# A hybrid SSD / short-convolution / MoE layer on one core: scale 2 and gate 2 summed on VectorE, their neighbours and the second C block moved in TensorE's order

## The chip, the cores and the metric

The kernel runs on one core of a Trainium2 chip. The time is the device time of the one launch, in microseconds (us), as the median of several runs. The profile is one more execution, recorded by the hardware profiler. In all rows PE is TensorE (matmul), PEld its weight load, DVE is VectorE, ACT is ScalarE, POOL is GpSimd, SP is SyncE, on whose queue (SPq) the large loads are issued.

## What is computed

One layer over 256 latent tokens (`x`) and 256 context tokens, model width 1024, all in float32. What matters here:

```
mod_x = (silu(c) @ w_mod + b_mod).reshape(6, D)       # 1024 -> 6 x 1024: shift 1, scale 1, gate 1, shift 2, scale 2, gate 2
hx    = rmsnorm(x) * (1 + scale1) + shift1
ox    = concat(bidirectional SSD scan, gated short conv)(hx @ w_in) @ w_out
x     = x + gate1 * ox
x     = x + gate2 * moe(rmsnorm(x) * (1 + scale2) + shift2)      # top 4 of 32 experts, w_gate_up 1024x2048, w_down 1024x1024 each
out   = rmsnorm(x)
```

`w_mod` is 1024 x 6144. It is used in three phases of 2048 columns: phase 0 holds shift 1 and scale 1, phase 1 gate 1 and shift 2, phase 2 scale 2 and gate 2. Gate 1, shift 2, scale 2 and gate 2 are wanted only behind the scan.

## The kernel before

The kernel runs in stages. Up to about 60 us the inputs are normalized and modulated and the first in-projection blocks are made. Then come the blocks of the scan's operands: X0 to X7 (`x_block`), B, and two C blocks (`c_block`, lines 531 to 536), each a projection with the weights split into a high and a low part (`split`, line 281: the high part a cast on ScalarE, the low part a subtraction on VectorE or GpSimd), 24 products on TensorE (`gemm`, line 291), and a convolution with silu (`conv_silu`, line 306: one operation on ScalarE, two additions on VectorE that read PSUM, a silu on ScalarE). The scan has 16 steps (the loop at line 676): step s is head pair s // 2 in direction s % 2. In each, `decays(s + 1)` makes the decay rows on TensorE, their exponentials on ScalarE, `mx` on VectorE and `ex` on GpSimd, and `outputs(s)` uses those of the step before on TensorE and, on odd steps, adds the result to `yb` on VectorE (line 614). Work that has nothing to do with the scan is put between as filler: the short-convolution blocks (`sc_block`, 12 of 24 in steps 2 to 13) and the modulation vectors. Behind the scan come the other 12 short-convolution blocks, the Z blocks, the out-projection, the router, and then the 32 experts, whose 12 MB of weights each are streamed through slots of 1 MB.

The modulation vectors of phases 1 and 2 are made by the generator `mods` (line 192). Each of its first eight `next` calls loads 128 rows of `w_mod` (1 MB, `load_mod`, line 187, in one of two slots of `ringm`) and multiplies them with 128 values of silu(c) on TensorE: four products 128x32 by 128x512, put side by side in one PSUM tile (line 202). The ninth call is the tail: 8 products with one column turn one half of the row into a column per partition (`pq`, line 211), and 2 of 512 columns copy the other half to all partitions (`pgate`, line 217). `m1` makes gate 1 and shift 2, `m2` scale 2 and gate 2. Calls of m1: three ahead of `token_steps` (line 649), two behind `scores(1)` (line 669), and, in the scan, one in each step from 2 to 5. Calls of m2: one in each step from 6 to 14.

What sets the order: TensorE's order is that of the program, written out (`manual_schedule`, line 405), from the end of the first projections to the end of the out-projection. The other engines and the DMA queues are put in order by the framework's planner, which goes by program order and by when it expects an operation to be ready; a queue, once planned, runs strictly in order. `tc.issue_after(i)` puts what is traced in it behind instruction i on that engine. A tile with a tag and `bufs=n` shares n buffers with all tiles of that tag, and waits until one is free. Those that matter: `proj` (PSUM, 2 buffers, the output of each projection block from X2 on), `cv` (2, a convolution's sum), `cx` (2, the X block in rows of channels, read by the token transposes), `ringm` (2 slots of 1 MB).

Silus from X1 on are held back behind `weighted`, the exponential at line 459, so that ScalarE's function table is loaded once.

Of the kernel before, what the change touches and what calls it, by code (L numbers as in the profile page):

```python
# [8 lines left out]
F32 = mybir.dt.float32  # L9
# [5 lines left out]
ALU = mybir.AluOpType  # L15
# [3 lines left out]
P = 128  # L19
D = 1024  # L20
KD = D // P
# [41 lines left out]
def body(ctx, tc, x, ctx_in, vectors_in, w_mod, b_mod, w_in, w_out, w_router, b_router, w_gate_up, b_gate_up,  # L63
         w_down, b_down, final_g, out, taps=None):
    nc = tc.nc
    taps = taps or {}

    def tap(name, ap):
        if name in taps:
            nc.gpsimd.dma_start(taps[name], ap)  # L70

    def dram(ap, offset, pattern):
        return bass.AP(tensor=ap.tensor, offset=ap.offset + offset, ap=pattern)
# [118 lines left out]
    def mods(ph, gate, gate_first, col):  # L192

        acc = ps.tile([P, 512], F32, tag="pm", bufs=1, name=f"pmod{ph}")
        rows = mp.tile([P, 512], F32, tag="sacc", name=f"rows{ph}")
        nc.gpsimd.memset(rows, 0.0)
        nc.gpsimd.dma_start(rows.rearrange("(j p) n -> j p n", p=32)[:, 0, :],
                            dram(b_mod, ph * 2048, [[512, 4], [1, 512]]))
        for k in range(KD):
            w = load_mod(ph, k)  # L200
            for j in range(4):
                nc.tensor.matmul(acc[32 * j:32 * j + 32, :], ct[:, k, :], w[:, 512 * j:512 * j + 512],
                                 start=(k == 0), stop=(k == KD - 1), skip_group_check=True)
            if k == KD - 1:
                nc.vector.tensor_add(rows, rows, acc)
            yield
        jg, jc = (0, 2) if gate_first else (2, 0)
        pq = ps.tile([P, 512], F32, tag="misc", bufs=2, name=f"pq{ph}")
        for q in range(KD):
            j = jc + q // 4  # L210
            nc.tensor.matmul(pq[:, q:q + 1], rows[:, (q % 4) * P:(q % 4 + 1) * P], ident[:, 32 * j:32 * j + 1],
                             start=True, stop=True)
        nc.vector.tensor_copy(col, pq[:, 0:KD])
        for hf in range(2):
            j = jg + hf
            pg = ps.tile([P, 512], F32, tag="misc", bufs=2, name=f"pgate{ph}_{hf}")
            nc.tensor.matmul(pg, ident[:, 32 * j:32 * j + 1].to_broadcast([P, P]), rows, start=True, stop=True)
            nc.scalar.copy(gate[:, hf, :], pg)
        yield

# [257 lines left out]
    g1 = mp.tile([P, 2, 512], F32, tag="g1", name="g1")  # L478
    g2 = mp.tile([P, 2, 512], F32, name="g2")
    m1 = mods(1, g1, True, sh2)  # L480
    m2 = mods(2, g2, False, gs2)
    yb = mp.tile([P, 8, T], F32, tag="x28", name="yb")
    ws = t2a.tile([P, 2, NT, NH, HD], F32, tag="big8", name="ws")
    xdt = t2a.tile([P, 2, NT, NH, HD], F32, tag="xd8", name="xdt")
# [46 lines left out]
    def c_block(g):  # L531
        if g == 0:
            wcol["C"] = load_cols(C0, "C")
        pp = proj(wcol["C"], g, T, f"C{g}", nc.vector)
        cch[g] = t2s.tile([P, T], F32, name=f"c{g}")
        conv_silu(pp, 10 + g, T, cch[g][:, None, :], weighted.ins)
# [56 lines left out]
    py = [None]  # L593

    def outputs(s_, mxs, exs):
        hp, d_ = s_ // 2, s_ % 2
        g = hp // 4
        ja, jb = (0, 1) if d_ == 0 else (1, 0)
        half = slice(P, T) if d_ == 0 else slice(0, P)
        xd = xdt[:, d_]  # L600
        if d_ == 0:
            py[0] = ps.tile([P, T], F32, tag="py", bufs=1, name=f"py{hp}")
        for hh in range(2):
            nc.tensor.matmul(py[0][64 * hh:64 * hh + 64, :], xd[:, ja, 2 * hp + hh, :], mxs[hh][:, 0:256],
                             start=(d_ == 0), stop=False, skip_group_check=True)
        for hh in range(2):
            nc.tensor.matmul(py[0][64 * hh:64 * hh + 64, half], xd[:, jb, 2 * hp + hh, :], mxs[hh][:, 256:384],
                             start=False, stop=False, skip_group_check=True)
        for hh in range(2):
            h_ = 2 * hp + hh  # L610
            nc.tensor.matmul(py[0][64 * hh:64 * hh + 64, :], h0[d_][g][:, (h_ % 8) * HD:(h_ % 8 + 1) * HD], exs[hh],
                             start=False, stop=(d_ == 1), skip_group_check=True)
        if d_ == 1:
            nc.vector.tensor_add(yb[:, hp, :], yb[:, hp, :], py[0])


    cs, cv = {}, {}
# [28 lines left out]
    context_b(1)  # L646
    x_block(3)
    c_block(0)
    for _ in range(3):
        next(m1)  # L650
    token_steps()
    x_tokens(0)
    x_tokens(1)
    decay_rows()
    c_block(1)
    x_block(4)
    x_tokens(2)
    x_tokens(3)
# [7 lines left out]
    last_silu = x_block(7)  # L666
    x_tokens(6)
    scores(1)
    for _ in range(2):
        next(m1)  # L670
    x_tokens(7)
    sc_steps = [(kind, 2 * q + half) for q in range(4) for kind in "CUB" for half in range(2)]
    fill = [lambda: context_state(0, 1), lambda: context_state(1, 1)]
# [2 lines left out]
    for s_ in range(16):  # L676
        if fill:
            fill.pop(0)()
        if s_ >= 2:
            next(m1 if s_ < 6 else m2, None)  # L680
        done_ = step
        if s_ < 15:
            step = decays(s_ + 1)
        outputs(s_, *done_)
    tap("y", yb)
    sa.close()
    scp = ctx.enter_context(tc.tile_pool(name="scp", bufs=1, reuse_waits="tile"))
# [7 lines left out]
    def sc_parts():  # L695
        while sc_done:
            ti, v_ = sc_done.pop(0)
            nc.scalar.copy(sc[0][:, ti, :], v_)
            nc.gpsimd.tensor_tensor(sc[1][:, ti, :], v_, sc[0][:, ti, :].bitcast(F32), op=ALU.subtract)

    sc_parts()
    for a in sc_steps[12:]:
        sc_block(*a)
        sc_parts()


    yhl = [scp.tile([P, 2, 4, T], F32R, tag=("ya", "yb")[g], name=f"y{g}") for g in range(2)]
# [770 lines left out]
```

## Time and profile before

| | us |
|---|---|
| median of 3 runs | 1299.02 (1299.01 to 1303.77) |
| the profiled execution | 1297.97 |
| its span, first to last instruction | 1296.2 |

| engine | busy, us | share of the span |
|---|---|---|
| TensorE | 1170.4 | 90% |
| VectorE | 435.6 | 34% |
| ScalarE | 258.4 | 20% |
| GpSimd | 122.1 | 9% |

The mean granted TensorE clock is 0.970. 466 MB are moved, 360 GB/s in the mean. The shares are means over stages of different kinds: up to 340 us TensorE works on projections and the scan while loads come and go, behind that the experts' weights are streamed. The rows further down are read by stage.

### The profile page before, as it was taken

The numbers are of one execution on the slowest core, as the hardware profiler recorded it, in microseconds if no ns is written. First come the engines' busy times: TensorE is split into PE (matmuls) and PEld (weight loads), VectorE is DVE, ScalarE is ACT, GpSimd is POOL, SyncE is SP. The second block draws the span as 40 slices with busy tenths as digits, with TensorE's granted clock in tenths as the row PEclk, the third lists the DMA queues.
The fourth block names the chain that finished last, engine by engine and source line by source line (L and its number), as shares of the span: only waits on it lengthen the run. The fifth ranks groups of instructions, "written<-read, shape, count | busy, mean of one in ns | idle before, by whom it ended". The sixth has DMA issues, their size and how long they took to land.

```text
span 1296.2 us, 16117 instructions
## 1 busy us (share of the span) xinstructions
PE 1170.4 (90%) x6113; PEld 538.1 (42%) x6113; DVE 435.6 (34%) x878; ACT 258.4 (20%) x510; POOL 122.1 (9%) x140
## 2 busy tenths in 40 slices
PE   7989999999899989899898878998977899888985
PEld 6666767988433322243222223422321243223221
DVE  5475454654432432213324212222321113212222
ACT  5444544554400010010001001000100010001002
POOL 1232333426100100000000000000000000000000
PEclk9999999999899999999999989999998999899998
DMA  9743468786499999999999999999999999999994
GB/s 324 266 164 130 164 228 280 257 294 270 170 417 415 416 415 417 416 416 417 417 416 416 416 416 416 416 416 416 416 416 417 417 416 417 416 416 416 416 415 186
DMA packets 111841, 466.12 MB, mean 360 GB/s; under 512 B 9576, under 2 KB 40424, under 8 KB 76944
## 3 DMA queue, kind: packets, MB, share of 16 engines
q1 hardware_dynamic: 111504, 464.37, 90.4%
q8 instruction: 50, 0.82, 0.3%
q0 software_dynamic: 256, 0.67, 0.1%
q14 instruction: 31, 0.25, 0.1%
HBM read 463.97 MB, written 1.05 MB: 359 GB/s over the span
## 4 chain that ended last, share of the span: by engine, by line
PE 77%; DMA 13%; DVE 6%; ACT 2%; issue 1%; SPq 1%; POOL 0%; ACTq 0%; DVEq 0%; POOLq 0%
PE pdn L1123 8%; PE pg L1111 8%; DMA gu<-in_w_gate_up_dram 8%; PE pl L1111 7%; PE pg L1191 6%; PE pc L1087 6%; PE pgl L1160 6%; PE pdn L1175 4%; PE pdn L1198 3%; DMA dn<-in_w_down_dram 3%; PE pd L999 2%; DMA wim<-in_w_mod_dram 2%; PE pgl L1154 1%; PE pat L1080 1%; PE ppX L293 1%; PE ppX L294 1%
## 5 line engine op out<-in xcount | busy, mean ns | idle before, releaser
L1111 PE MATMUL pg<-gu,xe 128*64 128x512 f32 x480 | 152.6, 610 | 1.5 <-DMA gu<-in_w_gate_up_dram 1.5
L1111 PE MATMUL pl<-gu,xe 128*64 128x512 f32 x480 | 149.3, 599 | 0.0
L1054 ACT ACTIVATE s<-a 128x512 f32<-128x512 f32 (+1 forms) x35 | 19.1, 545 | 591.0 <-DVE a L1053 591.0
L1087 PE MATMUL pc<-ye,gt 64*128 64x512 f32 (+1 forms) x248 | 100.3, 647 | 27.6 <-DVE ye L1134 14.5
L1160 PE MATMUL pgl<-gu,xe 128*32 128x512 f32 x896 | 114.4, 617 | 11.8 <-DMA gu<-in_w_gate_up_dram 11.8
L1123 PE MATMUL pdn<-dn,at 128*64 128x512 f32 x480 | 117.3, 634 | 6.9 <-ACT at L1082 6.8
L1089 DVE TENSOR_TENSOR x<-x,pc 128x512 f32<-128x512 f32 x124 | 81.7, 684 | 123.1 <-PE pc L1087 123.1
L1053 DVE TENSOR_SCALAR a<-pg 128x512 f32<-128x512 f32 x21 | 14.5, 690 | 216.0 <-PE pg L1111 150.5
L1191 PE MATMUL pg<-gu,xe 128*128 128x512 f32 x192 | 83.9, 592 | 0.0
L1134 DVE TENSOR_TENSOR ye<-g2s,pdn 128x512 f32<-128x512 f32 x29 | 19.9, 687 | 153.1 <-PE pdn L1123 106.3
L1313 POOL DMA_DIRECT2D fg<-in_final_g_dram x1 | 0.6, 591 | 746.4 <-PE pd L999 746.4
L1087 PEld LDWEIGHTS pc<-ye,gt 64*128 64x128 f32 (+1 forms) x248 | 28.5, 186 | 100.5 <-DVE x L1089 42.9
L1111 PEld LDWEIGHTS pl<-gu,xe 128*64 128x64 f32 x480 | 42.2, 138 | 67.1 <-issue 66.8
L1175 PE MATMUL pdn<-dn,at 128*32 128x512 f32 x448 | 63.4, 674 | 6.5 <-ACT at L1082 5.4
L1111 PEld LDWEIGHTS pg<-gu,xe 128*64 128x64 f32 x480 | 38.5, 138 | 69.9 <-issue 60.1
L1123 PEld LDWEIGHTS pdn<-dn,at 128*64 128x64 f32 x480 | 33.9, 145 | 72.8 <-issue 58.0
L1160 PEld LDWEIGHTS pgl<-gu,xe 128*32 128x32 f32 x896 | 24.9, 111 | 88.4 <-issue 56.7
L1191 PEld LDWEIGHTS pg<-gu,xe 128*128 128x128 f32 x192 | 35.8, 190 | 41.6 <-issue 40.9
L999 PE MATMUL pd<-oh,hr 128*128 128x256 f32 (+1 forms) x256 | 41.9, 305 | 5.6 <-DVE xe L1001 5.0
L1198 PE MATMUL pdn<-dn,at 128*128 128x512 f32 x96 | 43.5, 601 | 0.0
L999 PEld LDWEIGHTS pd<-oh,hr 128*128 128x128 f32 x256 | 34.2, 198 | 20.9 <-DVE xe L1001 10.7
L1067 DVE TENSOR_SCALAR go<-io,gp 128x128 f32<-128x128 f32 x56 | 18.6, 369 | 67.0 <-PE pgo L1071 67.0
(406 smaller groups left out, 1635.0 us busy)
## 6 DMA issues: line engine op xcount, KB each, us to landing
gu<-in_w_gate_up_dram SPq DMA_DIRECT2D x256, 1024.0 KB, 19.9
dn<-in_w_down_dram SPq DMA_DIRECT2D x127, 1024.0 KB, 20.0
wm<-in_w_mod_dram SPq DMA_DIRECT2D x16, 1024.0 KB, 5.2
wim<-in_w_mod_dram SPq DMA_DIRECT2D x8, 1024.0 KB, 11.6
wo<-in_w_out_dram SPq DMA_DIRECT2D x8, 1024.0 KB, 5.1
wiX<-in_w_in_dram SPq DMA_DIRECT2D x4, 1024.0 KB, 9.9
wiSC<-in_w_in_dram SPq DMA_DIRECT2D x4, 1024.0 KB, 6.4
wiSU<-in_w_in_dram SPq DMA_DIRECT2D x4, 1024.0 KB, 6.5
```

The source lines that it names most:

```text
L999: nc.tensor.matmul(pd[:, :width], hr[n // 2][:, n % 2, k * P:(k + 1) * P], oh[:, n % 2, :], start=(n == 0), stop=(n == 3))
L1054: nc.scalar.activation(s, a, AF.Sigmoid, scale=ALPHA)
L1067: nc.vector.tensor_scalar(go if cap == P else go.rearrange("p (a s) -> p a s", s=cap), io1 if cap == P else io1[:, None, 0:cap].to_broadca ...
L1087: nc.tensor.matmul(pc_, lhs, rhs, start=True, stop=True)
L1089: return nc.vector.tensor_add(ysl, ysl, pc_).ins
L1111: nc.tensor.matmul(pp[64 * hf:64 * hf + 64, :], xk[k], gu[k][:, i * FF + hf * 512:i * FF + hf * 512 + 512], start=False, stop=(k == KD - 1 ...
L1123: down = nc.tensor.matmul(pdn[64 * hf:64 * hf + 64, :], at[:, kk % 4, 64 * (kk // 4):64 * (kk // 4) + 64], dn[kk // 2][:, (kk % 2) * D + h ...
L1134: nc.vector.tensor_mul(ye, g2s, pdn)
L1160: nc.tensor.matmul(pgl[32 * q:32 * q + 32, :], xk[k], gv[:, :, 256 * q:256 * q + 256], start=False, stop=(k == KD - 1), skip_group_check=True)
L1175: down = nc.tensor.matmul(pdn[j:j + 32, :], at[:, c2, 32 * q:32 * q + 32], dn[q][:, c2 * D + hf * 512:c2 * D + hf * 512 + 512], start=(q = ...
L1191: nc.tensor.matmul(pgs[i][hf], xk[k], gu[k][:, i * FF + hf * 512:i * FF + hf * 512 + 512], start=False, stop=(k == KD - 1))
L1198: nc.tensor.matmul(pdn, ats[kk // 4][:, kk % 4, :], dn[kk // 2][:, (kk % 2) * D + hf * 512:(kk % 2) * D + hf * 512 + 512], start=(kk == 0) ...
```

## The change

Phase 1 (gate 1, shift 2) stays on TensorE in `mods`; only its bias rows are now filled and fetched behind the eight weight steps, in a call of their own. Phase 2 (scale 2, gate 2) is made by a new generator, `mods_by_rows`: each of the 128 partitions keeps its own sum of 2 x 1024 values in SBUF, to which VectorE adds 128 rows of `w_mod`, each times its value of silu(c) (two operations of 128x1024 for each of the eight loads); at the end TensorE sums over the partitions, with `onesf` in the place of the selecting columns. The sums are put behind the latest `yb` addition. In TensorE's order, the second C block goes from behind `decay_rows` to a place right behind the first; two calls of m1 stand ahead of `token_steps` in the place of three, none behind `scores(1)`, and six on the even steps 2 to 12; the eight weight calls of m2 stand at the end of the odd steps. The tail of m2 comes behind the first of the last 12 short-convolution blocks, the bias rows of m1 behind the third, and its tail behind the fifth.

```diff
 def mods(ph, gate, gate_first, col):
     acc = ps.tile([P, 512], F32, tag="pm", bufs=1, name=f"pmod{ph}")
-    rows = mp.tile([P, 512], F32, tag="sacc", name=f"rows{ph}")
-    nc.gpsimd.memset(rows, 0.0)
-    nc.gpsimd.dma_start(rows.rearrange("(j p) n -> j p n", p=32)[:, 0, :],
-                        dram(b_mod, ph * 2048, [[512, 4], [1, 512]]))
     for k in range(KD):
...
-            if k == KD - 1:
-                nc.vector.tensor_add(rows, rows, acc)
             yield
+        rows = mp.tile([P, 512], F32, tag="sacc", name=f"rows{ph}")
+        nc.gpsimd.memset(rows, 0.0)
+        nc.gpsimd.dma_start(rows.rearrange("(j p) n -> j p n", p=32)[:, 0, :],
+                            dram(b_mod, ph * 2048, [[512, 4], [1, 512]]))
+        nc.vector.tensor_add(rows, rows, acc)
+        yield
...
+    def mods_by_rows(ph, gate, gate_first, col):
+
+        sacc = mp.tile([P, 2, 512], F32, tag="sacc", name=f"sacc{ph}")
+        parts = (gate, sacc) if gate_first else (sacc, gate)
+        for h_, a in enumerate(parts):
+            nc.gpsimd.memset(a, 0.0)
+            nc.gpsimd.dma_start(a[0:1], dram(b_mod, ph * 2048 + h_ * 1024, [[0, 1], [512, 2], [1, 512]]))
+        for k in range(KD):
+            w = load_mod(ph, k)
+            with tc.issue_after(scanned[0]):
+                for j in range(2):
+                    a = parts[j].rearrange("p a n -> p (a n)")
+                    nc.vector.scalar_tensor_tensor(a, w[:, D * j:D * j + D], ct[:, k, 0:1], a,
+                                                   op0=ALU.mult, op1=ALU.add)
+            yield
+        pq = ps.tile([P, 512], F32, tag="misc", bufs=2, name=f"pq{ph}")
+        for q in range(KD):
+            nc.tensor.matmul(pq[:, q:q + 1], sacc[:, q // 4, (q % 4) * P:(q % 4 + 1) * P], onesf[:, 0:1],
+                             start=True, stop=True)
+        nc.vector.tensor_copy(col, pq[:, 0:KD])
+        for hf in range(2):
+            pg = ps.tile([P, 512], F32, tag="misc", bufs=2, name=f"pgate{ph}_{hf}")
+            nc.tensor.matmul(pg, onesf, gate[:, hf, :], start=True, stop=True)
             nc.scalar.copy(gate[:, hf, :], pg)
         yield
...
-    m2 = mods(2, g2, False, gs2)
+    m2 = mods_by_rows(2, g2, False, gs2)
...
-            nc.vector.tensor_add(yb[:, hp, :], yb[:, hp, :], py[0])
+            scanned[0] = nc.vector.tensor_add(yb[:, hp, :], yb[:, hp, :], py[0]).ins
...
     c_block(0)
-    for _ in range(3):
+    c_block(1)
+    for _ in range(2):
         next(m1)
     token_steps()
     x_tokens(0)
     x_tokens(1)
     decay_rows()
-    c_block(1)
     x_block(4)
...
     scores(1)
-    for _ in range(2):
-        next(m1)
     x_tokens(7)
...
-        if s_ >= 2:
-            next(m1 if s_ < 6 else m2, None)
+        if s_ in range(2, 14, 2):
+            next(m1)
...
         outputs(s_, *done_)
+        if s_ % 2:
+            next(m2)
...
-    for a in sc_steps[12:]:
+    for i_, a in enumerate(sc_steps[12:]):
         sc_block(*a)
         sc_parts()
+        if i_ in (0, 2, 4):
+            next(m1 if i_ else m2)
```

## Rows read from the trace of the kernel before

**Rows 1.** Busy us by engine in stretches, with clock, DMA share, GB/s.

```profile
core 0: us, PE busy (x) PEld busy (x) DVE busy (x) ACT busy (x) POOL busy (x), PEclk, DMA share, GB/s
122.32:217.25 94.93, 93.88 (x715) 63.69 (x713) 48.40 (x77) 49.80 (x124) 36.19 (x41) 1.00 0.67 227
...
346.00:1290.00 944.00, 845.50 (x3940) 285.59 (x3936) 246.94 (x510) 83.35 (x180) 6.94 (x7) 0.97 1.00 410
...
330.00:340.00 10.00, 6.61 (x34) 5.53 (x34) 6.57 (x29) 4.11 (x12) 0.00 (x0) 0.72 0.00 2
```

**Rows 2.** Waits of TensorE, 60 to 220 us: total, times, longest.

```profile
PE pmod L202 <- DMA wm<-in_w_mod_dram: 4.4, 1, 4.4
...
PE py L604 <- DVE mx L586: 0.4, 1, 0.4
```

**Rows 3.** The chain that ended last, steps 4 and 5: start, us, what.

```profile
146.56 0.96 PE ppSU L296 x8
147.52 1.00 PE pmod L202 x8
...
153.79 1.68 PE pq L211 x16
155.47 1.82 PE pgate L217 x4
```

**Rows 4.** VectorE's instructions by form, 120 to 240 us: total, mean ns.

```profile
L288 DVE TENSOR_TENSOR loSU<-wiSU,hiSU 128x1024 fp32r<-128x1024 f32 x7 | 8.6, 1225 | 14.9 <-ACT hiSU L287 14.9
```

**Rows 5.** Busy us by engine in scan steps 10 and 11 (U blocks).

```profile
186.47:199.01 12.54, 12.54 (x103) 8.72 (x102) 8.44 (x13) 5.89 (x14) 7.45 (x6) 1.00 0.75 252
```

**Rows 6.** ScalarE in order of time: start, us, what, idle before and releaser.

```profile
75.77 0.42 ACT L459 ACTIVATE wc<-wc 64x256 f32<-64x256 f32 x1 [3.67 <-DVE wc L458]
...
77.50 0.63 ACT L317 ACTIVATE cx<-cv 128x512 f32<-128x512 f32 x1
...
78.97 0.77 ACT L311 ACTIVATE cv<-ppX,vs 128x512 f32<-128x512 f32 x1
85.66 0.63 ACT L317 ACTIVATE cx<-cv 128x512 f32<-128x512 f32 x1 [5.92 <-PE px L519]
```

**Rows 7.** VectorE in order of time, ahead of the scan.

```profile
76.44 0.40 DVE L460 TENSOR_TENSOR wc<-wc,dtx 64x256 f32<-64x256 f32 x1
...
83.47 0.75 DVE L314 SCALAR_TENSOR_TENSOR cv<-ppX,vs,cv 128x510 f32<-128x510 f32 x1
...
87.65 0.48 DVE L314 SCALAR_TENSOR_TENSOR cv<-ppC,vs,cv 128x255 f32<-128x255 f32 x1
```

**Rows 8.** TensorE in order of time, ahead of the scan.

```profile
75.57 1.92 PE L202 MATMUL pmod<-wm,ct 128*32 128x512 f32 x16
81.89 1.93 PE L202 MATMUL pmod<-wm,ct 128*32 128x512 f32 x8 [4.39 <-DMA wm<-in_w_mod_dram]
...
88.79 0.40 PE L293 MATMUL ppX<-hhi,hiX 128*128 128x512 f32 x1
...
121.94 0.63 PE L519 MATMUL px<-ident,cx 128*128 128x128 f32 x4 [0.96 <-DVE ws L522]
```

**Rows 9.** TensorE in stretches: length, busy us, granted clock, DMA share, GB/s.

```profile
77.49:81.89 4.40, 0.01 (x2) 1.00 0.95 331
...
331.88:334.73 2.85, 0.34 (x4) 0.95 0.00 0
81.89:85.30 3.41, 3.41 (x18) 0.50 0.81 268
```

**Rows 10.** Loads of `wm`, 16 of them, issue to landing, in us.

```profile
DMA to landing us min/median/max: 4.7/5.2/8.4
```

**Rows 11.** VectorE's `mx` products and GpSimd's `ex` beside the second.

```profile
143.60 0.56 DVE L586 TENSOR_TENSOR mx<-mx,cbf 128x384 f32<-128x384 f32 x1 [0.96 <-ACT mx L583]
...
144.86 1.11 DVE L586 TENSOR_TENSOR mx<-mx,cbf 128x384 f32<-128x384 f32 x1
143.92 1.64 POOL L588 TENSOR_TENSOR ex<-ex,c 128x256 f32<-128x256 f32 x2 [4.42 <-ACT ex L585]
```

More of the change, by code (lines that the diff above doesn't have):

```diff
@@ L217, in mods @@
             nc.tensor.matmul(pg, ident[:, 32 * j:32 * j + 1].to_broadcast([P, P]), rows, start=True, stop=True)
+            nc.scalar.copy(gate[:, hf, :], pg)
+        yield
+    scanned = [None]
+    def mods_by_rows(ph, gate, gate_first, col):
[11 more added lines that the diff above has]
+                                                   op0=ALU.mult, op1=ALU.add)
+            yield
+        pq = ps.tile([P, 512], F32, tag="misc", bufs=2, name=f"pq{ph}")
[6 more added lines that the diff above has]
+            nc.tensor.matmul(pg, onesf, gate[:, hf, :], start=True, stop=True)
             nc.scalar.copy(gate[:, hf, :], pg)
```

## The prediction

> **What bounds the kernel now.** Read the stages first [rows 1]. From 346 us to the end the 16 DMA engines are busy 1.00 of the time and move 410 GB/s: the expert weights set the pace, not TensorE. That stream can't start earlier by itself. In the ten microseconds before the first expert the DMA engines move 2 GB/s, because all the slots are full and wait for the first expert to use them up. So the end moves one for one with the end of the part in front of it, and all of this change lies in that part. There the scan (122.32 to 217.25) is a TensorE stage: busy 93.88 of 94.93 us, against 48.40 for VectorE and 36.19 for GpSimd.
>
> Then read who waits [rows 2]. Between 60 and 220 us the largest wait of TensorE is 4.4 us, once, for a `wm` tile: the third `next(m1)` ahead of the scan. In the scan itself there is only 0.4 us, at the last step, for `mx`.
>
> Then the chain through one scan step [rows 3]. Each `next(m1)` or `next(m2)` with weights is 1.00 us of the chain, and each tail is 1.68 (`pq`) + 1.82 (`pgate`) = 3.50 us. Nothing hides them.
>
> **Part 1, scale 2 and gate 2 leave TensorE.** Before, 11 weight steps lie in the scan (3 of m1, 8 of m2). After, 6 do (m1 k = 2 to 7, on the even steps 2 to 12). That is 5 x 1.00 = 5.0 us off the chain [rows 3]. The three other m1 steps of before lie ahead of the scan and are costed in part 3.
>
> The two tails don't go away: they move from steps 5 and 14 to the blocks behind the scan. Those blocks are projections with TensorE at work all the time, so -7.0 and +7.0. The new forms have the same shapes: 8 products with one column, 2 with 512. Bounds: -0.5 to +1 for waits, for tail 2 needs the last sum on VectorE, and tail 1 the bias rows that GpSimd now fetches behind tail 2. One projection block of 24 products (8 of them 0.96 us [rows 3], so 2.9 us) lies ahead of the first and two behind the fetch of the second. I take 0.
>
> VectorE gets 16 operations of 128x1024 with two inputs in SBUF. The nearest row is the 128x1024 subtraction, 1.225 us [rows 4]: 19.6 us in all, 2.45 us every second step. A pair of steps becomes 12.54 - 1.0 = 11.5 us long. In the busiest pair, that with the two U blocks, VectorE is busy 8.44 of 12.54 us [rows 5]; it would then be busy 10.9 of 11.5. Everywhere else it has room. So I count them as hidden as long as the work behind them on VectorE has slack, and that it has in each step with a projection block: `mx` of step s+1 is made at the start of step s, and is wanted one block (2.9 us) later.
>
> The exception is the end. Steps 14 and 15 have no block, and tail 2 stood there before as cover. The sums of k = 6 come behind the `yb` add of step 13, ahead of step 15's `mx`, for which TensorE waits already [rows 2]. Bounds 0 (the planner puts them later) to 2.45 us (all of it shows). I take 1.8, nearer the upper end, since no work is left to hide it.
>
> What else moves: the loads are the same 16. The slots that m2 holds come free a few microseconds later, so the first two expert loads on SP's queue are later, as are the loads behind them. Those are wanted more than 15 us later, the experts at 340 us: nothing. GpSimd's two zero fills and two bias fetches for m2 need nothing and can run at the very start: nothing.
>
> **Part 2, the second C block ahead of the transposes.** This is where the rows speak against the change. TensorE's order is written out, so what its next item waits for holds all the rest. A projection needs one of the two `proj` buffers in PSUM. X2 and X3 hold them, C0 takes X2's, and C1 must take X3's. That is free only when X3's convolution has read it. Follow that in ScalarE's and VectorE's rows [rows 6, 7]: the weights' exponential ends at 76.2, a table load follows, X1's silu runs at 77.50 to 78.13 and frees the `cv` buffer that X3's convolution needs. ScalarE begins that at 78.97, ends it at 79.74, and VectorE's two additions take 2 x 0.75 us. Before, the second began at 83.47 and ended at 84.22, behind the subtraction for C1, and nothing on TensorE waited for it, since C1 stood behind the token transposes there. After, that subtraction stands earlier, so they can end at about 81.4 (80.5 if ScalarE takes X3 ahead of the cast for X4).
>
> So TensorE, done with C0 at 75.57 [rows 8], is idle to 81.4: 5.8 us instead of 4.4. Then it goes on at the lower clock. Before, after 4.40 us without work, the grant was 0.50, the 1.2 GHz level, for 3.41 us [rows 9]; that much time does half the work, 1.7 us lost. With it C1 takes 2.9 + 1.7 = 4.6 us to 86.0, two m1 steps 1.92 [rows 8] to 87.9, the step transposes 0.5, so the transposes of X0 (0.4) end at about 88.9.
>
> Now the next wait. X4 needs C0's `proj` buffer. C0's convolution needs a `cv` buffer that X2's silu frees, and that silu writes where X0's tokens lay: it waited for the transposes, 5.92 us, until 85.66 [rows 6]. C0's last addition ended at 88.13 [rows 7], 2.5 us after that silu began. Before, C1 filled that time, and X4 started at 88.79 with no wait [rows 8]. After, C1 has been used up in front. The silu begins at 89.2 (0.3 us for the signal, an estimate), the addition ends at 91.7, and TensorE, done with X1's transposes at about 89.4, stands idle until then. X4 starts at 91.8 or so instead of 88.79: **+3.1 us**. Bounds: +2.0 with the earlier cast order, +3.8 if VectorE's token products come between the additions.
>
> **Part 3, three m1 steps fewer ahead of the scan.** The third one and its 4.4 us wait are inside the interval just costed. The two behind `scores(1)` are worth nothing: TensorE waited for VectorE behind them anyway (0.96 us, until 121.94 [rows 8]), so without them the wait is 2.9 us long. Here the clock comes in. After 2.85 us with nearly no work at 331.88 the grant fell as well, to a mean of 0.95 in that stretch [rows 9]. The new gaps of 2.4 us (ahead of X4) and 2.9 us are of that size. Each costs 0 to 1.7 us. I take 0.7 in all: one of them, half hidden behind the waits for ScalarE and VectorE that open the scan.
>
> **The sum**, against the profiled execution's own 1297.97 us (span 1296.2 and 1.8 around it; the median of the runs is 1.05 us higher): -5.0 + 0 + 1.8 + 3.1 + 0.7 = +0.6, so 1298.6 us. The low ends give -5.0 - 0.5 + 0 + 2.0 + 0 = -3.5, 1294.5. The high ends give -5.0 + 1 + 2.45 + 3.8 + 3.4 = +5.7, 1303.6. What is won in the scan is given back ahead of it.
>
> **Rivals.**
> - C1 isn't held (the convolution of X3 comes early, or the buffer is another): C1 fills the wait as meant. Then C0 ends at 75.57, C1 2.9, m1 1.9, steps 0.5, X0's transposes 0.4 end at 81.3, and X4 starts 2.9 later at 84.2, 4.6 us earlier than before. With -5.0 and +1.8: -7.8, 1290.2 us. For it: the last input of the step transposes, `wc`, is ready at 76.84 [rows 7], so they would wait for nothing. Against it: the two buffers, and when ScalarE comes to X3 [rows 6].
> - The slot cycle (slower). There are two `wm` slots, m1 and m2 take them in turn. m2's is free only when both sums have read it, and the next load must land before the next pair's sums: 11.5 - 2.45 = 9.1 us. A load lands in 5.2 us, at most 8.4 [rows 10]. If it also stands behind another 1 MB load on SP (2.6 us at 410 GB/s), it takes 11.0 us; the sums then hold VectorE's queue with `mx` and the block splits behind them, and the pairs become 13.4 us long: 6 x 1.9 = 11.4 us more, 1310 us. It decides from 9.1 us on. Against it: the DMA engines are busy 0.67 in the scan [rows 1], so a load seldom meets another.
> - VectorE and GpSimd take turns. The row shows it: a 128x384 `mx` takes 0.56 us alone and 1.11 beside GpSimd's `ex` product [rows 11]. If all the new sums are doubled like that, VectorE is busy 8.44 + 4.9 = 13.3 us in a U pair of 11.5, 1.8 us too much in each of the two: 3.6 us, 1302.2. The Trainium skill, "SBUF — State Buffer", section "SBUF: two separate sides", speaks against this change: VectorE with two SBUF inputs and GpSimd share a port pair that one of them holds for a whole instruction. By that rule the trace agrees, with the 1.11 us, and the time would be this rival's. What speaks against it: behind `mx` GpSimd is idle in most steps, and the sums fall there.
>
> **How the numbers follow.** Forecast 0.62, C1 not held 0.17, slot cycle 0.11, taking turns 0.07, anything else 0.03. The predicted time is the forecast's, 1298.6. Its own range is 1294.5 to 1303.6. With the turns that is 0.69, so the range reaches down to take in the C1 rival, 1289.5 to 1304.0, and leaves out the slot cycle and the rest. 0.5% (6.5 us) is about what a measurement of this kernel can tell from no change. Faster by more: the C1 rival and half of the rest, 0.18. Slower by more: the slot cycle and half of the rest, 0.12. Within: 0.70.
>
> **What would show it.** In the changed kernel's trace: TensorE idle for 5 to 6 us behind C0, released by VectorE's addition for X3; a second gap ahead of X4, released by the addition for C0; odd scan steps of 5.3 us and even ones of 6.3 us with no wait in steps 2 to 13; a wait of about 2 us for `mx` at step 15; the first expert's products within a microsecond or two of where before has them. No gap behind C0, or an X4 that starts before 88 us, makes the prediction wrong on the fast side. Scan pairs over 12 us, or sums that wait for `wm`, make it wrong on the slow side.

## The result, and the profile after

The changed kernel takes 1307.7 us (median; 1305.39 to 1309.85) beside 1299.01 us for the kernel before (1298.58 to 1303.77). The ratio is 1.0055, 95% interval 1.0043 to 1.0067: slower, and 3.7 us above the upper end of the range. The profiled execution has a span of 1308.1 us, 11.9 longer than that of before; it is the longest run of the ten, so the shift of the medians, 8.7 us, is the better size. One of the ten executions of the run with two subtractions on VectorE (below) took 3967 us; that run's median counts it, its ratio does not.

In the changed kernel the lines from 293 to 614 stand 28 further down (293, 314, 498, 519, 614 are now 321, 342, 526, 547, 642), and 30 in those runs built on it that keep `added`, a record of each convolution's second addition; `mx` is at line 614, the sums on VectorE at line 235.

First the waits of TensorE from 60 to 220 us (total, times, longest), to be read beside [rows 2]:

```profile
PE ppC L321 <- DVE cv L342: 8.9, 1, 8.9
PE py L632 <- DVE mx L614: 2.9, 1, 2.9
PE px L547 <- DVE ws L550: 2.8, 1, 2.8
PE ppX L321 <- DVE cv L342: 1.9, 1, 1.9
PE py L632 <- DVE yb L642: 1.0, 1, 1.0
```

Each wait that was forecast is there: C1 behind X3's second addition, X4 behind C0's, X7's transposes, `mx` at the last step. But the first is 8.9 us where 5.8 was said, and the `yb` wait was in no part of the sum. TensorE's own rows at these places (start, us, what, idle before), beside [rows 8]:

```profile
84.84 0.55 PE L321 MATMUL ppC<-hhi,hiC 128*128 128x256 f32 x1 [8.93 <-DVE cv L342]
...
95.20 0.68 PE L321 MATMUL ppX<-hhi,hiX 128*128 128x512 f32 x1 [1.86 <-DVE cv L342]
95.68 0.63 PE L322 MATMUL ppX<-hlo,hiX 128*128 128x512 f32 x1
...
99.39 0.40 PE L322 MATMUL ppX<-hlo,hiX 128*128 128x512 f32 x1
...
130.02 1.09 PE L547 MATMUL px<-ident,cx 128*128 128x128 f32 x4 [2.81 <-DVE ws L550]
...
132.57 3.75 PE L573 MATMUL pst<-ws,bcT 128*128 128x512 f32 x4
```

X4 starts at 95.20 in the place of 88.79. X4's first products take 0.63 us, later ones 0.40, and the four products that open the scan 3.75 us. The granted clock of these stretches (columns as in [rows 1]) shows why:

```profile
79.50:83.20 3.70, 0.00 (x0) 0.00 (x0) 3.63 (x7) 0.49 (x1) 2.43 (x2) 0.50 0.79 269
84.80:92.60 7.80, 7.66 (x50) 5.81 (x50) 0.66 (x3) 1.06 (x2) 2.37 (x1) 0.77 0.13 26
95.00:101.00 6.00, 5.80 (x19) 4.64 (x20) 2.16 (x7) 1.06 (x3) 0.35 (x1) 0.72 0.89 333
130.00:138.00 8.00, 7.95 (x32) 4.25 (x32) 3.29 (x9) 5.20 (x13) 2.62 (x4) 0.61 0.25 85
210.00:220.00 10.00, 6.08 (x35) 3.08 (x31) 7.51 (x8) 3.75 (x13) 7.94 (x8) 0.74 0.68 238
```

The grant is at 0.50, the 1.2 GHz level, within C1's wait, and in part there again behind each of the three later waits: before X4, before the scan, and at its end.

What holds C1 is on VectorE, and beside it GpSimd (start, us, what), to be read with [rows 7]:

```profile
76.47 1.22 DVE L316 TENSOR_TENSOR loC<-wiC,hiC 128x1024 fp32r<-128x1024 f32 x1
...
77.95 1.33 DVE L524 CAST a<-acs 32x256 fp32r<-32x256 f32 x6
79.31 3.82 DVE L526 TENSOR_TENSOR a<-acs,a 32x256 fp32r<-32x256 f32 x6
83.16 0.75 DVE L340 SCALAR_TENSOR_TENSOR cv<-ppX,vs,cv 128x510 f32<-128x510 f32 x1
83.94 0.75 DVE L342 SCALAR_TENSOR_TENSOR cv<-ppX,vs,cv 128x510 f32<-128x510 f32 x1
...
79.50 2.42 POOL L316 TENSOR_TENSOR loX<-wiX,hiX 128x1024 fp32r<-128x1024 f32 x1
```

ScalarE's part of X3's convolution begins at 79.22 and takes 0.77 us, as forecast. But all twelve operations of `decay_rows` stand ahead of X3's additions in VectorE's queue, and the six subtractions among them take 3.82 us beside GpSimd's subtraction for X4.

In the kernel before, the same twelve stood ahead of X3's additions too. The subtraction for C1 came behind them there, and it was the one that fell beside GpSimd:

```profile
77.73 1.76 DVE L498 TENSOR_TENSOR a<-acs,a 32x256 fp32r<-32x256 f32 x6
79.52 3.25 DVE L288 TENSOR_TENSOR loC<-wiC,hiC 128x1024 fp32r<-128x1024 f32 x1
82.69 0.73 DVE L312 SCALAR_TENSOR_TENSOR cv<-ppX,vs,cv 128x510 f32<-128x510 f32 x1
...
79.23 2.46 POOL L288 TENSOR_TENSOR loX<-wiX,hiX 128x1024 fp32r<-128x1024 f32 x1
```

So with the subtraction for C1 in front X3's additions begin no earlier: at 83.16 us, before at 82.69.

In the scan, the chain that ended last (start, us, what):

```profile
144.38 0.96 PE ppSC L324 x8
145.34 0.99 PE pmod L198 x8
...
150.65 0.96 PE ppSC L324 x8
...
155.73 0.96 PE ppSU L324 x8
...
212.30 1.53 DVE sacc L235
213.83 1.67 DVE g L235
215.50 1.01 DVE mx L614
```

One step is 6.27 us, the next 5.08, the pair 11.35 (11.5 was said), and there is no wait until step 14. Then both sums of k = 6 and `mx` lie on the chain.

So, place by place in the two profiled executions (us; "later" is after less before, the forecast is the prediction's own sum carried along):

| place | before | after | later | forecast |
|---|---|---|---|---|
| X4's first product | 88.79 | 95.20 | +6.4 | +3.1 |
| X7's transposes | 121.94 | 130.02 | +8.1 | +3.1 |
| first short-convolution block in the scan, its last 8 products | 134.03 | 144.38 | +10.4 | +3.8 |
| first block behind the scan | 217.25 | 219.94 | +2.7 | -6.4 |
| out-projection | 279.01 | 289.37 | +10.4 | +0.6 |

The scan with its end won 7.7 us, not 10.2; the front lost 10.4, not 3.8. The two tails come back behind the scan (7.0, as said), which makes +10.4 at the out-projection. The other 1.5 us of this execution arise in the router: the same products run from 324.74 to 331.35 us before at a granted clock of 1.00, and from 335.11 to 343.27 now at 0.79. The first expert's products start at 351.70 in the place of 340.47. From there to the end it is 956.4 us, before 955.7, and 955.2 to 956.7 in all runs below.

### The profile page after: what moved, and what is told of

It reads as the page before. It is cut to its first block, busy times and chain, and to the rows that moved or that the text cites. A ratio compares the mean times of both kernels' runs of the same rounds, so it can differ in the third digit from the quotient of the medians.

```text
span 1308.1 us, 16010 instructions
## 1 busy us (share of the span) xinstructions
PE 1177.9 (90%) x6049; PEld 544.8 (42%) x6049; DVE 459.8 (35%) x893; ACT 258.9 (20%) x510; POOL 127.5 (10%) x142
## 4 chain that ended last, share of the span: by engine, by line
PE 70%; DMA 17%; DVE 8%; ACT 2%; issue 1%; SPq 1%; POOL 0%; ACTq 0%; DVEq 0%; POOLq 0%
DMA gu<-in_w_gate_up_dram 9%; PE pdn L1153 6%; DMA dn<-in_w_down_dram 6%; PE pg L1221 6%; PE pgl L1190 6%; PE pg L1141 6%; PE pc L1117 6%; PE pl L1141 6%; PE pdn L1205 4%; PE pdn L1228 3%; PE pd L1029 2%; DMA wim<-in_w_mod_dram 2%; PE pat L1110 1%; PE pgl L1184 1%; PE ppX L321 1%
## 5 line engine op out<-in xcount | busy, mean ns | idle before, releaser
L1153 PE MATMUL pdn<-dn,at 128*64 128x512 f32 x480 | 122.8, 659 | 6.9 <-ACT at L1112 6.8
```

The lines of the kernel that those rows point to most:

```text
L1153: down = nc.tensor.matmul(pdn[64 * hf:64 * hf + 64, :], at[:, kk % 4, 64 * (kk // 4):64 * (kk // 4) + 64], dn[kk // 2][:, (kk % 2) * D + h ...
```

## The experiments

The theory after the result: the front loses the time, and not because of TensorE's order by itself. C1 needs a `proj` buffer, that buffer waits for X3's additions, and those stand in VectorE's queue behind the decay rows, which GpSimd slows. The rivals: VectorE's queue holds X4 anyway, whatever C1 does; the sums on VectorE spoil the scan.

All ratios are to the kernel before, run beside on the same chip. The changed kernel's is 1.0055.

**C1 back behind the decay rows.**

```diff
     c_block(0)
-    c_block(1)
...
     decay_rows()
+    c_block(1)
```

> The changed kernel with the second C block put back behind decay_rows; all else as changed. Theory (the place of C1): C1 waits 8.93 us for X3's buffer in the changed kernel and X4 then waits again at the lower clock. With C1 back, TensorE goes from C0 through two m1 steps and the step transposes without a long wait, C1 starts near 84.5 and X4 near 88, in the place of 95.2: 7 to 9 us less, 1299 to 1301 us. Rival (the sums on VectorE are what costs): C1's place moves a wait from one place to another, and the time stays at 1305 or above.

Measured: 1300.5 us, ratio 1.0009 [1.0000, 1.0019]. The place of C1 is worth some 6 us. But a wait remains, with another name. TensorE's longest wait:

```profile
PE px L547 <- DVE dtc L501: 6.3, 1, 6.3
```

and VectorE in order of time:

```profile
79.62 3.25 DVE L316 TENSOR_TENSOR loC<-wiC,hiC 128x1024 fp32r<-128x1024 f32 x1
```

C1 starts at 85.73, where before has 85.84. X4 starts at 91.00, still 2.2 later than before, because C1 runs at the lower clock here (0.50 from 85 to 91 us; before 1.00 from 85.30 on). X1's transposes now wait for the token copies `dtc`, which stand in VectorE's queue behind the decay rows, that subtraction for C1 (3.25 us here, where [rows 4] has 1.225) and X3's additions. So from 79 to 85 us VectorE's queue is what TensorE waits for. The 4.4 us wait for `wm` in the kernel before [rows 2] lay over the same stretch.

**The decay rows held behind X3's second addition** (`added[3]`), C1 left where the change puts it.

```diff
-    decay_rows()
+    with tc.issue_after(added[3]):
+        decay_rows()
```

> The changed kernel with decay_rows (12 small VectorE operations, 5.2 us in the changed kernel's trace) held behind X3's second addition; C1 stays early. Theory (the planner's order on VectorE makes the difference between the 5.8 us that was forecast for C1's wait and the 8.93 measured): C1 starts at about 81.5 in the place of 84.84, X4 at about 92, and the time is 3 to 4 us less, 1304 us. Rival (ScalarE or the buffer itself holds C1): C1 starts at 84 or later and the time stays within 1 us of 1307.7.

Measured: 1303.86 us, ratio 1.0032 [1.0015, 1.0050]. C1's wait is now the one forecast:

```profile
PE ppC L321 <- DVE cv L344: 5.8, 1, 5.8
```

So of the 8.9 us, 3.1 come from the decay rows ahead of X3's additions. X4 starts at 93.61, later than the 92 expected. This is the order that the prediction's 81.4 us needs.

**Two m1 steps back behind `scores(1)`**, in the gap ahead of X7's transposes.

```diff
     scores(1)
+    for _ in range(2):
+        next(m1)
     x_tokens(7)
...
-        if s_ in range(2, 14, 2):
+        if s_ in range(2, 10, 2):
```

> The changed kernel with the two m1 steps put back behind scores(1), and two fewer in the scan (k = 4 to 7 on steps 2, 4, 6, 8). Theory (they were cover, and kept the clock): the wait ahead of X7's transposes falls from 2.8 to 1.0 us, the clock stays at its upper level at the scan's start (2.3 us back), and the scan has two steps less (2.0 us): 4 us less, 1303.5 us. Rival (the clock falls for another reason, and the steps cost there what they cost in the scan): within 1 us of 1307.7.

Measured: 1305.51 us, ratio 1.0049 [1.0032, 1.0066]. By the medians that is about half of what was expected, by the ratio less, and the interval takes in the change's 1.0055: the time alone does not tell this run from the change. In the trace the front behaves: the wait ahead of X7's transposes is 1.0 in the place of 2.8, and the clock is kept. The same ten microseconds in the changed kernel and in this run, in this order:

```profile
130.00:140.00 10.00, 9.95 (x37) 5.12 (x37) 4.13 (x10) 5.95 (x15) 4.30 (x5) 0.69 0.20 68
```

```profile
130.00:140.00 10.00, 9.31 (x56) 4.91 (x55) 5.04 (x12) 7.96 (x21) 4.50 (x7) 1.00 0.67 264
```

But the end of the scan takes part of it back: with no weight step on steps 10 and 12 VectorE falls behind there, and the `yb` waits grow from 1.0 us to 2.1 (the `mx` wait is 2.7).

```profile
PE py L632 <- DVE mx L614: 2.7, 1, 2.7
PE py L632 <- DVE yb L642: 2.1, 2, 1.9
```

**The last two sums behind the scan.**

```diff
-        if s_ % 2:
+        if s_ % 2 and s_ < 13:
             next(m2)
+    for _ in range(2):
+        next(m2)
```

with each tail two blocks later.

> The changed kernel with the sums of k = 6 taken from step 13 and done with those of k = 7 behind the scan, and the tails two blocks later. Theory (the two sums ahead of step 15's mx hold TensorE, 2.9 + 1.0 us, and the clock falls there): the waits at the last step go back to about 0.4 us and the first block behind the scan runs at the upper clock: 3.5 to 5 us less, 1303 to 1304 us. Rival (the sums only move behind the scan, where the block splits wait for VectorE): 1306 to 1308.

Measured: 1304.96 us, ratio 1.0036 [1.0022, 1.0050]. A little above the 1303 to 1304 expected. The wait for `mx` is gone; that for `yb`, 1.0 us, stays. So that wait is not the sums': step 14 has nothing left to put between, where tail 2 stood before. The two runs below that leave both tails in the scan (the order of VectorE's queue, the front alone) do not have it.

**The order of VectorE's queue alone, in the kernel before.** No sums on VectorE; the decay rows behind C1's second addition (`added[11]`).

```diff
-    for _ in range(3):
+    for _ in range(2):
         next(m1)
...
-    decay_rows()
     c_block(1)
+    with tc.issue_after(added[11]):
+        decay_rows()
...
-            next(m1 if s_ < 6 else m2, None)
+            next(m1 if s_ < 7 else m2, None)
```

> The kernel before with only the order of the front changed, no sums on VectorE: two m1 steps ahead of the step transposes in the place of three, m1's k = 4 to 7 and its tail on scan steps 2 to 6, m2 one step later each; C1 stays behind X0's and X1's transposes; decay_rows stands behind C1, and its operations on VectorE are held behind C1's second addition. Theory (VectorE's queue, not TensorE, sets when X4 starts): the copies of the token products follow X3's additions directly, by about 81.5 us, so X0's transposes go then, C0's and C1's additions are early, and X4 starts at about 86 us in the place of 88.79: -2.8. One weight step more in the scan is +1.0. Sum -1.8: 1297.3 us, ratio 0.9986. Rival (TensorE and the landing of the wm tile set the front, VectorE only follows): X4 at 87.8 or later, and a new wait for the decay rows at scores, 1 us: 1299.3 or more, ratio 1.000 to 1.002.

Measured: 1298.45 us, ratio 0.9991 [0.9982, 1.0001], between the two. X4 starts at 87.14 (86 was expected) and X7's transposes at 120.34, 1.6 us before [rows 8]; the first block behind the scan starts at 215.89, so 1.4 of it is left there, with one weight step more in the scan. A gain of that size is not told from none by the ratio; the start times in the trace tell it.

**The sums alone, with the front of before.**

```diff
-    m2 = mods(2, g2, False, gs2)
+    m2 = mods_by_rows(2, g2, False, gs2)
...
-        if s_ >= 2:
-            next(m1 if s_ < 6 else m2, None)
+        if s_ in (4, 10, 12):
+            next(m1)
...
+        if s_ % 2 and s_ < 13:
+            next(m2)
+    for _ in range(2):
+        next(m2)
...
```

> The sums on VectorE alone, with the front of the kernel before: three m1 steps ahead of the step transposes, C1 behind decay_rows, two m1 steps behind scores(1). In the scan m1's k = 5 to 7 stand on steps 4, 10 and 12 and m2's sums on the odd steps 1 to 11; k = 6 and 7 of m2 come behind step 15; the tails stand behind the scan. So only 3 weight steps of TensorE lie in the scan in the place of 11. Theory (the scan part won what was forecast, and the front alone lost it): -8.0 for the steps, +1.0 to +1.5 for the end of the scan (the wait for the last addition to yb, the first softmax products behind it), 0 for the front and no clock loss ahead of the scan: 1292.3 us, ratio 0.995. Rival (VectorE is the bound of the scan once the weight steps no longer cover it): steps 10 to 13 wait for mx and the gain is halved, 1296 us, ratio 0.9975.

Measured: 1292.38 us, ratio 0.9944 [0.9927, 0.9961]. The rival, that VectorE bounds the scan, falls: the waits of TensorE between 60 and 225 us name `mx` nowhere.

```profile
PE pmod L198 <- DMA wm<-in_w_mod_dram: 4.0, 1, 4.0
PE py L632 <- DVE yb L642: 1.0, 1, 1.0
```

**The front alone, with all sums on TensorE.** C1 right behind C0, two and two m1 steps ahead of the scan, and k = 4 to 7 in it.

```diff
     c_block(0)
-    for _ in range(3):
+    c_block(1)
+    for _ in range(2):
         next(m1)
...
     decay_rows()
-    c_block(1)
...
-            next(m1 if s_ < 6 else m2, None)
+            next(m1 if s_ < 7 else m2, None)
```

> The change's front on the kernel before, with all sums on TensorE as before: C1 right behind C0, two m1 steps ahead of the step transposes and two behind scores(1), m1's k = 4 to 7 and its tail on steps 2 to 6, m2 one step later each. Theory (C1's place by itself makes the loss): C1 is held about 9 us behind C0, X4 starts at about 95 us in the place of 88.79 (+6.3), runs at the lower clock (+1.7), and one weight step more lies in the scan (+1.0): 1308 us, ratio 1.007. Rival (the hold was long only with what else the change moved, the sums' zero fills and bias fetches on GpSimd's queue ahead of it): the hold is 5.8 us as forecast and X4 starts at about 91.8: 1303, ratio 1.003.

Measured: 1307.01 us, ratio 1.0057 [1.0040, 1.0074]. C1's wait is the same without anything of `mods_by_rows`:

```profile
84.51 0.55 PE L293 MATMUL ppC<-hhi,hiC 128*128 128x256 f32 x1 [8.94 <-DVE cv L314]
```

X4 starts at 95.82, and the lag is 8.7 us at the scan's first short-convolution block and 9.0 behind the scan, so the weight step more in the scan costs little.

These two runs show the sign of the parts: the sums in this form win 0.56%, C1's place loses 0.57%. They do not add up to the change's 1.0055, which has three weight steps more in the scan than the run with the sums alone, its last sums at the scan's end, and the gap ahead of X7's transposes unfilled.

**Both repairs**: the front of the run on VectorE's order, and the scan of the run with the sums alone with one more m1 step in it (on steps 4, 6, 10 and 12). Against the run with the sums alone:

```diff
-    for _ in range(3):
+    for _ in range(2):
         next(m1)
...
-    decay_rows()
     c_block(1)
+    with tc.issue_after(added[11]):
+        decay_rows()
...
-        if s_ in (4, 10, 12):
+        if s_ in (4, 6, 10, 12):
             next(m1)
```

> The front of the run with decay_rows behind C1 and the scan of the run with the sums alone: two m1 steps ahead of the step transposes, two behind scores(1), m1's k = 4 to 7 on steps 4, 6, 10 and 12. If both theories hold they add: -2.8 at X4, -7.0 in the scan (4 weight steps in the place of 11), +1.0 to +1.5 at its end: about 1290.8 us, ratio 0.9935. If the gain of the front is lost again ahead of the scan (X7's transposes wait for VectorE as long as they did at 121.94), X4's 2.8 us show up as a longer wait there and it is 1293.5, ratio 0.9955.

Measured: 1291.27 us, ratio 0.9940 [0.9924, 0.9957]. The first sum had 0.9935 and the second 0.9955; the interval holds both, and also the 0.9944 of the sums alone, so the time does not show that the gains add. The trace speaks for the first sum: X4 starts at 86.84, and what it wins is still there at the scan (X7's transposes at 120.02, in the run with the sums alone at 123.43).

**C1 in a buffer of its own**, in the changed kernel (`proj` takes the tag of the buffer as an argument):

```diff
-        pp = proj(wcol["C"], g, T, f"C{g}", nc.vector)
+        pp = proj(wcol["C"], g, T, f"C{g}", nc.vector, "py" if g else "proj")
```

> The changed kernel, with C1's product in PSUM's buffer of the scan's outputs (tag py, unused there until the scan) in the place of one of the two proj buffers; nothing else is changed. Theory (the shared proj buffer is what holds C1): C1 starts with no wait right behind C0 at about 75.8 us and X4 takes X3's buffer; X0's and X1's transposes then wait for VectorE's queue (decay rows, X3's additions, the token copies, to about 85.3), and X4 starts at about 86 us in the place of 95.2: -9, and its cold 1.7 us go too, while the wait ahead of X7's transposes takes back up to 2: 1297 to 1299 us, ratio 0.998 to 1.000. Rival (VectorE's queue alone sets X4's start and the buffer only shows its wait earlier): X4 at 91 us as in the run with C1 back behind the decay rows, 1300.5 to 1303 us, ratio 1.001 to 1.003.

Measured: 1301.82 us, ratio 1.0019 [1.0008, 1.0031], 4.7 us better than the change by the ratios. The buffer is what holds C1: no wait of C1 is left. But X4 starts at 88.26, between the 86 of the theory and the 91 of the rival, and the time is in the rival's band. VectorE, GpSimd and TensorE:

```profile
79.12 6.16 DVE L526 TENSOR_TENSOR a<-acs,a 32x256 fp32r<-32x256 f32 x6
85.31 0.75 DVE L340 SCALAR_TENSOR_TENSOR cv<-ppX,vs,cv 128x510 f32<-128x510 f32 x1
...
79.32 4.80 POOL L316 TENSOR_TENSOR loX<-wiX,hiX 128x1024 fp32r<-128x1024 f32 x2
...
87.52 1.09 PE L547 MATMUL px<-ident,cx 128*128 128x128 f32 x4 [5.79 <-DVE dtc L501]
```

With C1 early, GpSimd has two subtractions to do at that time (X4 and X5), and the six small ones on VectorE take 6.16 us.

**Those two subtractions on VectorE**, the rest as in the run before this one:

```diff
-        pp = proj(wcol["X"], half, 512, f"X{ti}", nc.gpsimd) if q else pps[2 + half]
+        pp = proj(wcol["X"], half, 512, f"X{ti}", nc.vector if ti in (4, 5) else nc.gpsimd) if q else pps[2 + half]
```

> The changed kernel with C1 in the buffer py, with one edit: the subtractions that make the low parts of X4's and X5's weights run on VectorE in the place of GpSimd, so that GpSimd has no two-input operation beside the decay rows; VectorE gets 2 x 1.2 us more work. Theory (VectorE and GpSimd hold each other up: the six subtractions of the decay rows took 6.16 us there beside GpSimd and 1.76 in the kernel before): the six take about 1.8 us again, X3's additions end 2 to 4 us earlier in spite of the added work, and X4 starts at about 84.5 to 86 us in the place of 88.3: 1298 to 1300 us, ratio 0.9995 to 1.001. Rival (they are slow for another reason, such as their 32-partition operands): they stay at 6 us, the added subtraction comes on top, and X4 starts at 89.5 or later, 1303 us or more, ratio 1.003.

Measured: 1297.72 us, ratio 0.9983 [0.9973, 0.9992], below the band expected, on the theory's side.

```profile
78.96 1.67 DVE L526 TENSOR_TENSOR a<-acs,a 32x256 fp32r<-32x256 f32 x6
...
81.33 1.22 DVE L316 TENSOR_TENSOR loX<-wiX,hiX 128x1024 fp32r<-128x1024 f32 x1
...
85.01 1.09 PE L547 MATMUL px<-ident,cx 128*128 128x128 f32 x4 [3.45 <-DVE dtc L501]
```

The six take 1.67 us again, and X4 starts 2.5 us earlier (85.75) though VectorE does 2.4 us more work ahead of it. So it is the two engines side by side that made them slow, not their shape.

**C1 in its own buffer with the better scan, the decay rows held in two places.** First behind X3's second addition, against the run with both repairs:

```diff
     c_block(0)
+    c_block(1)
     for _ in range(2):
         next(m1)
...
-    c_block(1)
-    with tc.issue_after(added[11]):
+    with tc.issue_after(added[3]):
         decay_rows()
```

> The run with both (its scan, its two and two m1 steps ahead), with C1 right behind C0 in the buffer py and the operations of decay_rows held behind X3's second addition. Theory: X3's additions then end at about 80.5 to 81.5, the token copies follow, X4 starts at about 83 us in the place of 85.9: -2.9, of which the wait for X7's transposes may take back 1 to 2: 1288.5 to 1290.5 us, ratio 0.992 to 0.993. Rival (the front is then bound by the X blocks' own chain of silu, transposes and token products, so that an earlier X4 only waits further on): 1291.3 us as there, ratio 0.994.

Measured: 1291.76 us, ratio 0.9948 [0.9931, 0.9965]; neither the theory's 83 us nor a wait further on, but X4 at 88.59. The decay rows now stood between X3's additions and the token copies, still beside GpSimd's pair, and even the six casts took 3.75 us:

```profile
81.61 3.75 DVE L526 CAST a<-acs 32x256 fp32r<-32x256 f32 x6
85.38 1.67 DVE L528 TENSOR_TENSOR a<-acs,a 32x256 fp32r<-32x256 f32 x6
87.09 0.42 DVE L502 COPY dtc<-pc 128x256 f32<-128x256 f32 x1
```

Then one edit:

```diff
-    with tc.issue_after(added[3]):
+    with tc.issue_after(added[11]):
         decay_rows()
```

> The run with C1 in the buffer py and the scan of the run with both, with one edit: the operations of decay_rows are held behind C1's second addition in the place of X3's. Theory (VectorE's queue holds X1's transposes, and it is the decay rows in front of the token copies that did it, 5.4 us of them): X3's additions end at about 81.6, the token copies at 82.3, the wait for dtc falls from 5.8 us to about 1, and X4 starts at about 83 to 84 us in the place of 88.6. If that is carried to the scan: 1287 us, ratio 0.991. Rival (an X4 this early only waits for its own chain further on, since X2's and X3's silus, transposes and products have to follow one another): at most half of it arrives, 1289.5 us or more, ratio 0.993 or more.

Measured: 1286.41 us, ratio 0.9894 [0.9877, 0.9911]: 1.06% faster than the kernel before, the fastest of all.

```profile
80.35 0.75 DVE L342 SCALAR_TENSOR_TENSOR cv<-ppX,vs,cv 128x510 f32<-128x510 f32 x1 [2.01 <-ACT cv L341]
...
79.72 4.72 POOL L316 TENSOR_TENSOR loX<-wiX,hiX 128x1024 fp32r<-128x1024 f32 x2
...
82.55 0.63 PE L549 MATMUL px<-ident,cx 128*128 128x128 f32 x4 [0.31 <-DVE dtc L503]
...
82.94 0.47 PE L321 MATMUL ppX<-hhi,hiX 128*128 128x512 f32 x1
...
117.09 0.63 PE L549 MATMUL px<-ident,cx 128*128 128x128 f32 x4 [0.96 <-DVE ws L552]
```

X4 starts 5.65 us before that of the other place, and X7's transposes (122.78 there) 5.7: all of it arrives at the scan. What now stands beside GpSimd's pair on VectorE, X3's additions and the token copies and products, reads PSUM and takes no longer than elsewhere. The rival, a chain of the X blocks that would swallow it, falls.

## Why the prediction was wrong

It was wrong in sizes, on the slow side; no rival came true in the place where it was written down.

1. **That the stream of experts only starts later or earlier with what is in front.** Right: 955.2 to 956.7 us from its first product to the end in every profile.
2. **The scan.** Right: no wait in steps 2 to 13. A weight step less was worth 1.19 us, not 1.00 (a pair of 11.35 us in the place of 12.54): 0.9 us more in all five. No sum waited for `wm`, so the slot cycle did not come about. The sums took 1.27 us each as a rule where 1.225 was taken [rows 4].
3. **C1's hold.** The wait and its place were right, the term was mis-sized: +6.4 at X4 in the place of +3.1. The step that failed is "After, that subtraction stands earlier, so they can end at about 81.4". X3's additions ended at 84.69, where before has 84.22. The step took the subtraction for C1 for what holds X3's additions. But the decay rows stand ahead of them as well, in both kernels, and whichever of these operations falls beside GpSimd's subtraction for X4 is held: before it was the one for C1, now the six small ones. So the same work took about as long in either order (76.23 to 82.69 us before, 76.47 to 83.16 after). With the decay rows held back the wait was 5.8 us, the forecast's own number, and the time 1303.86 us.
4. **VectorE and GpSimd take turns.** This rival had the right mechanism in the wrong place. It was priced for the sums in the scan, where most of the sums fall into GpSimd's idle time as said (1.39 and 1.34 us in the mean). In the front it was not looked for: 3.82 us for six subtractions that take 1.67 alone. The trace of before had the sign of it, the 3.25 us of C1's subtraction, where [rows 4] has 1.225. The Trainium skill, "SBUF — State Buffer", section "SBUF: two separate sides", says that the one of the two that starts first has the shared ports for its whole instruction while the other is blocked; the traces agree, for GpSimd's subtraction took 2.35 to 2.46 us in each case and only VectorE's grew.
5. **The clock.** +0.7 was taken, of bounds 0 to 3.4. In the profiled execution it was about 4.0: 1.7 between X4 and X7's transposes (from 6.4 to 8.1 in the table; eight products 0.43 us apart where 0.23 is usual make 1.6 of it) and 2.3 at the opening of the scan (from 8.1 to 10.4). The second is more than usual: in the five runs with the same wait of 2.8 us ahead of X7's transposes it was 0.8 to 1.1. So both gaps that were forecast cost the clock, 2.6 us as a rule, and "one of them, half hidden" was too little. Filling the second kept the clock, as the third run shows.
6. **The end of the scan.** +1.8 was taken, of bounds 0 to 2.45; it cost about 5.2 (12.0 and the 0.9 of point 2 were to be won ahead of it, 7.7 arrived). The sums are 3.2 us of the chain, not 2.45, since they stood beside GpSimd's work; the wait for `yb`, 1.0, was left out, though the prediction itself named tail 2 as the cover there; the rest goes with the clock of 0.74 in that stretch.
7. **The tails behind the scan.** Right: 7.0 given back there, and what came with them no more than 0.7.

Three terms were short by much the same: the hold by 3.3 us, the clock by 3.3 in this execution (1.9 as a rule), the end of the scan by 3.4. With the sizes as measured the sum is: front +10.4, scan and its end -7.7, tails and what follows +7.7, in all +10.4 at the out-projection. The router's 1.5 us and some 1.4 at the scan's opening are this execution's own, and make most of the 3.2 by which it exceeds the shift of the medians. The run at 0.9944 has the sums without this front, fewer weight steps in the scan and the last sums behind it; the front was never needed for them.

## What to carry to other kernels

Before a block is moved earlier on the bottleneck engine, list what has to free its buffer, and then what the queue of the engine that frees it will hold in the new order: in-order queues make the small operations ahead of it the price, here 3.1 us for twelve of them. Taking one operation out from between is worth nothing if the others then take its place beside a busy neighbour. Look at the same microseconds on the engine that shares ports with it. Where several changes come as one, time the parts: here one part, tried alone, won 0.56% and the other lost 0.57%, and the place of one helper's twelve operations in VectorE's queue decided another 5.4 us.

## What the runs showed of the hardware

Six VectorE subtractions of 32 partitions, 1.67 us in all, took 3.82 us beside one GpSimd subtraction of 2.42 us and 6.16 beside two (4.80 us). The growth, 2.15 and 4.49, is nearly GpSimd's whole time, so these short operations did not slip in between. Casts, with one input, are held as well: six took 3.75 us where they take 1.13 to 1.33. Additions that read PSUM are not: X3's took 0.75 us each beside GpSimd's pair in the last run, as elsewhere. Giving VectorE the work of GpSimd, 2.4 us more, made VectorE's queue shorter.

The same wait does not always cost the same clock. Behind the 2.8 us ahead of X7's transposes TensorE lost 2.3 us in one profile and 0.8 to 1.1 in five. In the router, where it waits 0.83 and some 1.13 us in every profile, the grant was 0.79 in the changed kernel's and 1.00 in that of before, 8.16 us in the place of 6.61.
